# Moving the weights' split tiles, the pairs inside them and the sums of x to other places modulo 256 bytes

## The chip, the cores and the metric

One NeuronCore of a Trainium2 chip runs the whole kernel. The metric is the device time of one execution in microseconds (us), as the median of several executions. TensorE (PE in the profile) multiplies matrices: a weight load (LDWEIGHTS, shown as PEld) puts the stationary operand, 128 columns, into the array, and the MATMUL then streams the moving operand past it, 256 or 512 columns here. Both operands are read from SBUF, the on-chip memory of 128 partitions; an address below is a byte address within a partition. VectorE is DVE, ScalarE is ACT, GpSimd is POOL, and SyncE (SP) issues nearly all DMAs.

## The reference, cut to what matters

The input x is 256 tokens by 4096. The work is two normalisations, one big projection, a gated convolution, windowed attention, and one output projection:

```python
def hybrid_layer(x, w_in, conv_w, sink, w_out, ln_g, ln_b):
    p = x @ w_in                      # 256x4096 @ 4096x13312
...
    y_conv = c_b * centred_short_conv(c_c * c_h, conv_w) * jax.nn.silu(c_z)
    y_attn = banded_window_attention(a_q, a_k, a_v, sink) * jax.nn.silu(a_z)
    y = jnp.concatenate([y_conv, y_attn], axis=-1) @ w_out   # 4096x4096
    return layer_norm(DN_ALPHA * x + y, ln_g, ln_b)
```

All is float32. The projections hold nearly all of the arithmetic.

## The kernel before, in words

**How a product is made.** A float32 number is split in two float32r halves, a rounded one (hi) and the rest (lo), and a product is three matmuls: x-hi by w-hi, x-hi by w-lo, x-lo by w-hi. The tokens are the stationary operand, 128 at a time; the weights are the moving operand. Each of the 8.8 thousand matmuls has a weight load of its own. The tokens' halves lie in `xT`, 32 blocks of 2048 bytes, one for each 128 rows of the weights (`kt`), in each the 256 tokens' hi and then their lo, so a stationary block starts at a multiple of 512 bytes from the start of `xT`.

**The weights** come by DMA in tiles of 8192 bytes per partition (`w0` to `w2`, later `w6` to `w8` and parts of `R`). ACT makes the hi half of a tile (`split_hi`, tile `whi`) and DVE the lo half (`split_lo`, tile `wlo`), three buffers each, three steps ahead of the matmuls that use them. The code lists the order by hand: a list of steps, with a function for each that is emitted in the order of the list, so nothing is left to a scheduler.

**Three kinds of step.** A whole piece (lines 242 to 244 in the input projection, 908 to 910 in the output projection) multiplies four blocks of 512 columns by both token halves: 24 matmuls of 512 columns. A "half" step is the same with two blocks. In the last two chunks of the output projection (`CHUNKS` is 512 seven times and 256 twice) the blocks are 256 columns wide, on the same lines 908 to 910. A pair step (`mm_pair`, lines 266 to 268) does two blocks of 512 columns with seven products instead of eight, by a Strassen-like scheme: the DMA brings four blocks of 256 columns, DVE adds three or four more from them (`sums`, lines 181 to 183), and 21 matmuls of 256 columns follow. Of their stationary blocks three of seven are blocks of `xT` in the input projection's pairs, or four, and the others are sums of token blocks, kept in the tiles `SC`, `SC2` and, in the output projection, `SCy`.

**Where the tiles lie.** Pools take SBUF in the order in which they are opened, each tile rounded up to 32 bytes. `const` holds `ident`, `cw`, `sk`, `xT`, `musd` (32 bytes) and `eps_t` (4 bytes); behind it lie `wpool` (`whi`, `w0` to `w2`, `wlo`), then `small`, then the pools opened later: `psc` with the sums of x, `pw`, `pa` or `pc` (attention's tiles, convolution's tiles), `p2`. In a pair step the eight blocks of 1024 bytes lie at the tile's start plus 0 to 7 times 1024; block 0 of `whi` and `wlo` is not written, since block 0 only serves the sums (`part`, line 189).

Worked out from the code, the starts modulo 256 are: `ident` and `xT` 128; `whi`, `wlo`, `w0` to `w2` 192; `SC`, `SC2`, `SCy`, `R`, `w6` to `w8` and all of attention's tiles (`kT`, `v`, `qhl`, `pT`, `z`, `p`) 224.

Other matmuls: attention's scores (lines 551 to 553: moving `kT`, stationary `qhl`) and outputs (606 to 608: moving `pT`, stationary `v`), the first two pieces (line 369: `first` by `hT`, in plain float32, which takes two passes), and transposes (lines 334, 352, 481, 592: moving `ident`, stationary the tile that is turned).

Of the kernel before, what the change touches and what calls it, by code (L numbers as in the profile page):

```python
# [8 lines left out]
F32 = mybir.dt.float32  # L9
F32R = mybir.dt.float32r  # L10
AF = mybir.ActivationFunctionType
ALU = mybir.AluOpType
AX = mybir.AxisListType

P = 128
# [25 lines left out]
HW = W // 2  # L41
# [6 lines left out]
OP = 4  # L48
OUT_ORDERS = ["s" * 8] * 2 + ["sSsSsSsSss"] * 5 + ["", ""]
N_W = 3  # L50


def units(ci):
# [32 lines left out]
def npairs(ci):  # L86
    return PAIRS[ci] if ci < OUT else OUT_ORDERS[ci - OUT].count("S")
# [11 lines left out]
def encoder_kernel(ctx: ExitStack, tc: tile.TileContext, x, emb_g, emb_b, wi, ws, conv_w, sink, wo, ln_g, ln_b, out):  # L99
    nc = tc.nc  # L100
    PSUM = bass.MemoryType.PSUM

    const = ctx.enter_context(tc.tile_pool(name="const", bufs=1))
    wpool = ctx.enter_context(tc.tile_pool(name="wpool", bufs=3))
    small = ctx.enter_context(tc.tile_pool(name="small", bufs=4))
# [13 lines left out]
    is_pair = lambda j: steps[j][0] in ("pair", "opair")  # L119

    raw, wh, wl = {}, {}, {}
# [6 lines left out]
    def w_bufs(j):  # L128

        bs = [(wpool, f"w{k}") for k in range(N_W)] + (extra if j < N_IN else [])  # L130
        if j >= N_IN and R is not None:
            late = j > in_R[0][0]
            bs += [(None, name) for last, name in in_R if j <= last and late == (name == "R2")]
        last_user = lambda b: max(u for c, u in user.items() if c == b or b[1] == "R2" and c[0] is None) if (
            b in user or b[1] == "R2") else -1
        return min((last_user(b), k) for k, b in enumerate(bs)), bs

    def load(j, to=None):
        kind, a, b = steps[j]
        if to is None:  # L140
            (_, k), bs = w_bufs(j)
            pool, name = bs[k]
            user[bs[k]] = j
            if pool is None:
                to = raw[j] = {"R0": R[:, 0, D // 2:D], "R1": R[:, 1, D // 2:D], "R2": R[:, :, 3 * D // 4:D]}[name]
            else:
                to = raw[j] = pool.tile([P, PIECE], F32, name=name, bufs=1)
        src = {"in": (wi, IN_PIECES), "out": (wo, OUT_PIECES)}.get(kind, (ws, ALL_PAIRS))
        src = src[0][src[1].index((a, b))]
        if len(to.shape) == 3:  # L150
            if is_pair(j):
                nc.sync.dma_start(out=to[:, 0, :], in_=src)
            else:
                nc.sync.dma_start(out=to, in_=src.rearrange("p (i n) -> p i n", i=2))
        else:
            nc.sync.dma_start(out=to[:, 0:src.shape[1]], in_=src)

    def loads(j):

        nonlocal nxt  # L160
        while nxt < len(steps) and nxt <= j + 7:
            (u, _), bs = w_bufs(nxt)
            if u > j + (2 if len(bs) > N_W else 3):
                break
# [20 lines left out]
    def part(j, t):  # L185

        if len(raw[j].shape) == 3:
            return t if len(t.shape) == 3 else t.rearrange("p (i n) -> p i n", i=2)
        return t[:, HW:] if is_pair(j) else t[:, 0:4 * HW] if steps[j][0] == "half" else t

    def half_tile(j, name):
        if j < len(steps) - 1:
            return wpool.tile([P, PIECE], F32R, name=name)
        (_, k), bs = w_bufs(j)
        user[bs[k]] = j
        return bs[k][0].tile([P, PIECE], F32R, name=bs[k][1], bufs=1)

    def split_hi(j):
        wh[j] = half_tile(j, "whi")
        nc.scalar.activation(part(j, wh[j]), part(j, raw[j]), AF.Copy)  # L200

    def split_lo(j):
        wl[j] = half_tile(j, "wlo")
        nc.vector.tensor_tensor(part(j, wl[j]), part(j, raw[j]), part(j, wh[j]).bitcast(F32), op=ALU.subtract)  # L204
        raw.pop(j)

    def split(j):
        if j < len(steps):
            split_hi(j)
            split_lo(j)  # L210
# [7 lines left out]
    sk = const.tile([P, HEADS], F32, name="sk")  # L218

    xT = const.tile([P, KT, 2 * S], F32R, name="xT")  # L220
    musd = const.tile([P, 2, 4], F32, name="musd")
    eps_t = const.tile([P, 1], F32, name="eps_t")
    nc.vector.memset(eps_t, LN_EPS)


    acc = {}
# [21 lines left out]
    def mm_pair(j):  # L248


        _, ci, p = steps[j]
        hi, lo = (t.pop(j).rearrange("p (b w) -> p b w", w=HW) for t in (wh, wl))
        last = p == npairs(ci) - 1
        if p == 0:
            for k in range(2):
                pacc[ci, k] = ps_p.tile([P, 2, HW], F32, name="pacc")
        a, b = 2 * p, 2 * p + 1
        x = lambda kt, i: (xT[:, kt, i * HT:(i + 1) * HT], xT[:, kt, (2 + i) * HT:(3 + i) * HT])
        sc = lambda n: (SC[p][:, 0, n, :], SC[p][:, 1, n, :])
        p0, p1, c0, c1 = pacc[ci, 0], pacc[ci, 1], acc[ci, 0], acc[ci, 1]  # L260
        for (ah, al), w, o, opens, closes in (
                (x(a, 0), 2, p0[:, 0, :], True, False), (x(b, 0), 3, c0[:, 0:HW], False, False),
                (sc(2), 1, c0[:, HW:W], False, False), (x(b, 1), 7, c1[:, 0:HW], False, False),
                (sc(0), 5, p1[:, 1, :], True, False), (x(a, 1) if ci < OUT else sc(3), 6, p0[:, 1, :], False, True),
                (sc(1), 4, p1[:, 0, :], False, True)):
            nc.tensor.matmul(o, ah, hi[:, w, :], start=(opens and p == 0), stop=False)  # L266
            nc.tensor.matmul(o, ah, lo[:, w, :], start=False, stop=False)  # L267
            nc.tensor.matmul(o, al, hi[:, w, :], start=False, stop=(closes and last))  # L268


    def small_chain(i, dst):
# [10 lines left out]
    with tc.tile_pool(name="pro", bufs=1) as pro:  # L282
# [27 lines left out]
        nc.sync.dma_start(out=sk, in_=bass.AP(tensor=sink.tensor, offset=sink.offset, ap=[[0, P], [1, HEADS]]))  # L310
        for j in range(4, 2 + N_W):
            load(j)
# [89 lines left out]
        transp2(2, (1,))  # L402
        turned1(1, 0, t1[0])
        split_hi(2)
        first_mm(0, 1)
        transp2(3, (1,))
        turned1(1, 1, t1[1])
        first_mm(1, 1)
        turned2(2)
        split_lo(2)  # L410
        load(5)
        x_split(2)
# [380 lines left out]
    for j in range(n_pro, N_IN):  # L793
        kind, ci, q = steps[j]
        if j == z0 + 4:
            extra.clear()
        if j == z0 + 12:
            extra.insert(0, (pw, "w6"))
        mm_pair(j) if kind == "pair" else mm(j)
        split_hi(j + 3)  # L800
        for fn, a in later.pop(j, []):
            fn(*a)
        if kind == "pair" and q == PAIRS[ci] - 1:
            pair_copy(ci)
            at(j + 1, pair_sums, ci)
        if j in X_SUMS:
            x_sums(X_SUMS.index(j), pa.tile([P, 4 * S], F32, name="xs", tag="zT", bufs=2))
        if steps[j + 1][1] != ci or j == N_IN - 1:
            if ci == c_ch0:
                at(j + 10, open_pc)  # L810
            if PAIRS[ci]:
                at(j + (4 if j < N_IN - 1 else 1), chunk_end, j + 1, ci)
            else:
                chunk_end(j, ci)
        loads(j)
        sums(j + 4)
        split_lo(j + 3)
# [180 lines left out]
    for n, (c0, w, pk, j0) in enumerate(chunks):  # L998
        us = out_units(n)
        np_ = sum(u[0] == "opair" for u in us)  # L1000
        for t, (kind, _, q) in enumerate(us):
            j = j0 + t
            if kind == "opair":
                mm_pair(j)
            else:
                mm_out(j, n, (0,) if n == ncs - 1 else (0, 1))
# [114 lines left out]
```

## Time and profile before

| | us |
|---|---|
| median of 3 runs (lowest, highest) | 1534.17 (1534.01, 1534.74) |
| span of the profiled execution | 1532.5 |
| PE busy in it | 1518.5, 8879 matmuls |
| PEld busy | 1330.7 |
| DVE busy | 1329.9 |
| ACT busy | 780.7 |

The page gives the span, from the first to the last instruction; what lies around the span in the profiled execution is not listed apart, and the median of the runs stands 1.7 us above the span. PE is busy in every slice and its granted clock is 1.000. A MATMUL's listed duration includes its tail in the array, in which the next one has long begun (0.39 us for one that is followed after 0.23 us), so sums of durations say little; what counts is the distance from one start to the next, read from the timeline. Start times there are given to 0.01 us, so a distance is taken over many matmuls in a row.

### The profile page before, as it was taken

The page shows a single profiled execution, that of the slowest core. Times are in us where ns is not written, and L with a number is a line of the kernel's source. Part 1 is how long each engine was busy: PE and PEld are TensorE (multiplying, and loading weights), DVE is VectorE, ACT ScalarE, POOL GpSimd, SP SyncE. Part 2 cuts the span into 40 slices and gives each one's busy share as a digit, 9 for nine tenths or more (in the row PEclk, how much of TensorE's full clock was granted, in tenths as well). Part 3 has the DMA queues.
Part 4 walks back from the last instruction along what each step waited for, and adds up shares of the span by engine and source line. Part 5 has one row for each costly group of instructions (what it writes and reads, how often), then busy time and mean ns, then how long its engine had stood idle before and what let it go on. Part 6 is the DMA issues. An engine that isn't in the chain of part 4 may idle for free.

```text
span 1532.5 us, 21818 instructions
## 1 busy us (share of the span) xinstructions
PE 1518.5 (99%) x8879; PEld 1330.7 (87%) x8879; DVE 1329.9 (87%) x1555; ACT 780.7 (51%) x669; POOL 1.3 (0%) x7
## 2 busy tenths in 40 slices
PE   7999999999999999999999999999999999999998
PEld 4888889989998988889888889888988888888897
DVE  7769889899899898898898999989898688888876
ACT  4545546656566555545455445544456344443431
POOL 0000000000000000000000000000000000000000
PEclk9999999999999999999999999999999999999999
DMA  7545554555555555656555555556557756666663
GB/s 290 205 179 192 207 197 163 204 179 203 203 177 181 183 178 205 231 185 234 188 190 208 209 195 196 204 183 228 206 193 287 268 188 226 250 206 225 213 239 140
DMA packets 71716, 315.65 MB, mean 206 GB/s; under 512 B 8544, under 2 KB 12608, under 8 KB 50880
## 3 DMA queue, kind: packets, MB, share of 16 engines
q1 hardware_dynamic: 70608, 312.43, 57.2%
q10 hardware_dynamic: 1008, 1.84, 0.3%
q8 instruction: 69, 1.13, 0.3%
q14 instruction: 31, 0.25, 0.0%
HBM read 305.23 MB, written 8.91 MB: 205 GB/s over the span
## 4 chain that ended last, share of the span: by engine, by line
PE 96%; DVE 2%; DMA 1%; ACT 0%; SPq 0%; issue 0%; ACTq 0%
PE acc L242 15%; PE acc L243 15%; PE acc L244 15%; PE acc L908 6%; PE acc L910 6%; PE acc L909 6%; PE pacc L267 6%; PE pacc L266 6%; PE pacc L268 5%; PE acc L267 4%; PE acc L266 4%; PE acc L268 4%; PE att L481 1%; DVE wlo L204 1%; DMA w<-in_ws 0%; DVE st L319 0%
## 5 line engine op out<-in xcount | busy, mean ns | idle before, releaser
L200 ACT ACTIVATE whi<-w 128x2048 fp32r<-128x2048 f32 (+1 forms) x354 | 621.3, 1755 | 628.1 <-DVE w L183 213.5
L204 DVE TENSOR_TENSOR wlo<-w,whi 128x2048 fp32r<-128x2048 f32 (+1 forms) x354 | 736.5, 2083 | 129.3 <-ACT whi L200 128.8
L242 PE MATMUL acc<-whi,xT 128*128 128x512 f32 x988 | 391.1, 396 | 0.0
L243 PE MATMUL acc<-wlo,xT 128*128 128x512 f32 x988 | 387.6, 392 | 0.0
L244 PE MATMUL acc<-whi,xT 128*128 128x512 f32 x988 | 386.2, 391 | 0.0
L244 PEld LDWEIGHTS acc<-whi,xT 128*128 128x128 f32 x988 | 185.6, 188 | 41.5
L243 PEld LDWEIGHTS acc<-wlo,xT 128*128 128x128 f32 x988 | 185.6, 188 | 38.2 <-DVE wlo L204 1.7
L242 PEld LDWEIGHTS acc<-whi,xT 128*128 128x128 f32 x988 | 185.7, 188 | 36.1
L908 PE MATMUL acc<-whi,xT 128*128 128x512 f32 (+1 forms) x480 | 176.0, 367 | 0.0
L910 PE MATMUL acc<-whi,xT 128*128 128x512 f32 (+1 forms) x480 | 175.2, 365 | 0.0
L909 PE MATMUL acc<-wlo,xT 128*128 128x512 f32 (+1 forms) x480 | 174.6, 364 | 0.2 <-DVE wlo L204 0.2
L181 DVE TENSOR_TENSOR w<-w 128x512 f32<-128x512 f32 x179 | 122.3, 683 | 8.7 <-DMA w<-in_ws 8.7
L910 PEld LDWEIGHTS acc<-whi,xT 128*128 128x128 f32 x480 | 90.1, 188 | 15.7
L909 PEld LDWEIGHTS acc<-wlo,xT 128*128 128x128 f32 x480 | 90.1, 188 | 15.5 <-DVE wlo L204 0.9
L267 PE MATMUL acc<-wlo,xT 128*128 128x256 f32 x370 | 103.3, 279 | 0.0
L266 PE MATMUL acc<-whi,xT 128*128 128x256 f32 x370 | 103.1, 279 | 0.0
L268 PE MATMUL acc<-whi,xT 128*128 128x256 f32 x370 | 103.1, 279 | 0.0
L908 PEld LDWEIGHTS acc<-whi,xT 128*128 128x128 f32 x480 | 90.2, 188 | 14.0 <-issue 0.4
L266 PE MATMUL pacc<-whi,xT 128*128 128x256 f32 x350 | 99.4, 284 | 0.0
L267 PE MATMUL pacc<-wlo,xT 128*128 128x256 f32 x350 | 97.8, 279 | 0.0
L268 PE MATMUL pacc<-whi,xT 128*128 128x256 f32 x350 | 97.6, 279 | 0.0
L267 PE MATMUL pacc<-wlo,SC 128*128 128x256 f32 x330 | 93.0, 282 | 0.0
(230 smaller groups left out, 2055.2 us busy)
## 6 DMA issues: line engine op xcount, KB each, us to landing
w<-in_wi SPq DMA_DIRECT2D x112, 1024.0 KB
w<-in_ws SPq DMA_DIRECT2D x202, 512.0 KB
w<-in_wo SPq DMA_DIRECT2D x41, 1024.0 KB
R<-in_wo SPq DMA_DIRECT2D x13, 1024.0 KB
x<-in_x SPq DMA_DIRECT2D x7, 512.0 KB
yl<-yd SPq DMA_DIRECT2D x7, 512.0 KB
xc<-in_x SPq DMA_DIRECT2D x14, 256.0 KB
R<-in_ws SPq DMA_DIRECT2D x6, 512.0 KB
```

Of the source, the lines that this page charges most:

```text
L181: nc.vector.tensor_tensor(s01, b22, b12.to_broadcast([P, 2, HW]), op=ALU.add)
L200: nc.scalar.activation(part(j, wh[j]), part(j, raw[j]), AF.Copy)
L204: nc.vector.tensor_tensor(part(j, wl[j]), part(j, raw[j]), part(j, wh[j]).bitcast(F32), op=ALU.subtract)
L242: nc.tensor.matmul(a, xh, hk, start=(first and k == 0), stop=False)
L243: nc.tensor.matmul(a, xh, lk, start=False, stop=False)
L244: nc.tensor.matmul(a, xl, hk, start=False, stop=(last and k == PK - 1))
L266: nc.tensor.matmul(o, ah, hi[:, w, :], start=(opens and p == 0), stop=False)
L267: nc.tensor.matmul(o, ah, lo[:, w, :], start=False, stop=False)
L268: nc.tensor.matmul(o, al, hi[:, w, :], start=False, stop=(closes and last))
L908: nc.tensor.matmul(o, yh, hk, start=first, stop=False)
L909: nc.tensor.matmul(o, yh, lk, start=False, stop=False)
L910: nc.tensor.matmul(o, yl, hk, start=False, stop=last)
```

## The change

Three things are done, and no instruction is added, removed or moved: on every engine the same instructions stand in the same order with the same waits, and only addresses differ.

- `musd` and `eps_t` go from `const` to `small`, which takes 64 bytes from in front of `wpool`: `whi` and `wlo` (and `w0` to `w2`) now start at 128 modulo 256, as `xT` does.
- An unused tile `gap` of 160 bytes in `small`, with the two tiles that moved there, moves every later pool up by 160 bytes: `SC`, `SC2`, `SCy`, `R`, `w6` to `w8` and attention's tiles go from 224 to 128 modulo 256.
- A pair's halves are written `SHIFT` = 48 elements, 192 bytes, lower in their tile than before (`dst`): block w then starts at the tile's start plus 1024 w minus 192, which is 192 modulo 256, where it was before. `mm_pair` reads blocks by `w - 1` from a view that starts there. The branch for a raw tile with two rows is taken by no pair step of this kernel: all 3885 matmuls of the pairs read at 192 modulo 256.

The offset of the moving block from the stationary block, modulo 256, is then:

| matmuls | lines before | offset before | offset after |
|---|---|---|---|
| 512 columns, `whi`/`wlo` by `xT` | 242 to 244, 908 to 910 | 64 | 0 |
| pairs, by `xT` | 266 to 268 | 64 | 64 |
| pairs, by `SC`, `SC2`, `SCy` | 266 to 268 | 224 | 64 |
| 256 columns of the last two chunks | 908 to 910 | 64 | 0 |
| attention | 551 to 553, 606 to 608 | 0 | 0 |
| transposes of tiles at 224 | 352, 481, 592 | 160 | 0 |

`first` by `hT` (line 369) goes from 224 to 0. 

```diff
+SHIFT = 48
...
+    def dst(j, t):
+
+        return t[:, HW - SHIFT:8 * HW - SHIFT] if is_pair(j) and len(raw[j].shape) == 2 else part(j, t)
...
     def split_hi(j):
         wh[j] = half_tile(j, "whi")
-        nc.scalar.activation(part(j, wh[j]), part(j, raw[j]), AF.Copy)
+        nc.scalar.activation(dst(j, wh[j]), part(j, raw[j]), AF.Copy)
 
     def split_lo(j):
         wl[j] = half_tile(j, "wlo")
-        nc.vector.tensor_tensor(part(j, wl[j]), part(j, raw[j]), part(j, wh[j]).bitcast(F32), op=ALU.subtract)
+        nc.vector.tensor_tensor(dst(j, wl[j]), part(j, raw[j]), dst(j, wh[j]).bitcast(F32), op=ALU.subtract)
+        if is_pair(j):
+            c0 = HW if len(raw[j].shape) == 3 else HW - SHIFT
+            wh[j], wl[j] = wh[j][:, c0:c0 + 7 * HW], wl[j][:, c0:c0 + 7 * HW]
         raw.pop(j)
...
     xT = const.tile([P, KT, 2 * S], F32R, name="xT")
-    musd = const.tile([P, 2, 4], F32, name="musd")
-    eps_t = const.tile([P, 1], F32, name="eps_t")
+    musd = small.tile([P, 2, 4], F32, name="musd", bufs=1)
+    eps_t = small.tile([P, 1], F32, name="eps_t", bufs=1)
     nc.vector.memset(eps_t, LN_EPS)
+    small.tile([P, 40], F32, name="gap", bufs=1)
...
-            nc.tensor.matmul(o, ah, hi[:, w, :], start=(opens and p == 0), stop=False)
-            nc.tensor.matmul(o, ah, lo[:, w, :], start=False, stop=False)
-            nc.tensor.matmul(o, al, hi[:, w, :], start=False, stop=(closes and last))
+            nc.tensor.matmul(o, ah, hi[:, w - 1, :], start=(opens and p == 0), stop=False)
+            nc.tensor.matmul(o, ah, lo[:, w - 1, :], start=False, stop=False)
+            nc.tensor.matmul(o, al, hi[:, w - 1, :], start=False, stop=(closes and last))
```

## The prediction

> **What bounds the kernel now.** First the page's busy times and the chain that ended last.
>
> ```profile
> PE 1518.5 (99%) x8879; PEld 1330.7 (87%) x8879; DVE 1329.9 (87%) x1555; ACT 780.7 (51%) x669; POOL 1.3 (0%) x7
> PE 96%; DVE 2%; DMA 1%; ACT 0%; SPq 0%; issue 0%; ACTq 0%
> ```
>
> TensorE is the bound: 96% of the chain is PE. The view of waits says whether PE is held up by anyone.
>
> ```profile
> ACT whi L200 <- PE acc L244: 176.9, 80, 3.9
> PE att L382 <- DMA x<-in_x: 8.7, 1, 8.7
> ```
>
> The longest wait of PE in that view is 8.7 us, once, at the start. The other way round, ACT waits 176.9 us for PE to free the hi tiles, so the splits run ahead of the matmuls. A saving in the distance between two matmuls is therefore a saving in time, until DVE is late. How near DVE is, by stage:
>
> ```profile
> core 0: us, PE busy (x) PEld busy (x) DVE busy (x) ACT busy (x) POOL busy (x), PEclk, DMA share, GB/s
> 330.00:600.00 270.00, 269.65 (x1693) 242.46 (x1692) 248.04 (x319) 162.35 (x186) 0.00 (x0) 1.00 0.53 184
> 600.00:1160.00 560.00, 560.00 (x3400) 499.90 (x3399) 508.22 (x556) 287.00 (x194) 0.00 (x0) 1.00 0.58 207
> ```
>
> DVE is busy 248 of 270 us in the attention stage and 508 of 560 in the convolution stage. PE could become 8% faster there before DVE's work alone is longer.
>
> So the question is the distance from one matmul to the next. The listing by form gives the counts of the 512-column matmuls.
>
> ```profile
> L242 PE MATMUL acc<-whi,xT 128*128 128x512 f32 x988 | 391.1, 396 | 0.0
> L243 PE MATMUL acc<-wlo,xT 128*128 128x512 f32 x988 | 387.6, 392 | 0.0
> L244 PE MATMUL acc<-whi,xT 128*128 128x512 f32 x988 | 386.2, 391 | 0.0
> L908 PE MATMUL acc<-whi,xT 128*128 128x512 f32 x368 | 144.8, 393 | 0.0
> L910 PE MATMUL acc<-whi,xT 128*128 128x512 f32 x368 | 144.3, 392 | 0.0
> L909 PE MATMUL acc<-wlo,xT 128*128 128x512 f32 x368 | 143.6, 390 | 0.2 <-DVE wlo L204 0.2
> ```
>
> These are 3 x 988 + 3 x 368 = 4068 matmuls. The timeline of PE gives their distance, here from the first and last row of two undisturbed stretches.
>
> ```profile
> 192.89 0.40 PE L242 MATMUL acc<-whi,xT 128*128 128x512 f32 x1
> 203.85 0.40 PE L244 MATMUL acc<-whi,xT 128*128 128x512 f32 x1
> 1187.24 0.40 PE L909 MATMUL acc<-wlo,xT 128*128 128x512 f32 x1
> 1263.70 0.39 PE L910 MATMUL acc<-whi,xT 128*128 128x512 f32 x1
> ```
>
> From 1187.24 to 1263.70 there are 334 distances: 228.9 ns each, and nearly all stretches show this number. The stretch from 192.89 to 203.85, with 47 distances at the same offset, shows 233.2. What would it be without any disturbance? The plain float32 matmuls take the same 512 columns in two passes:
>
> ```profile
> 23.65 3.60 PE L369 MATMUL acc<-first,hT 128*128 128x512 f32 x8
> 27.09 0.60 PE L352 MATMUL att<-ident,x 128*128 128x128 f32 x4
> ```
>
> Eight of them take 3.44 us, 430 ns each. Half of it, 215 ns, is my estimate of 512 columns streamed once with nothing in the way: 0.42 ns a column. So each 512-column matmul carries about 14 ns too much, 57 us in all. The 256-column matmuls, in the same view:
>
> ```profile
> 457.69 0.28 PE L606 MATMUL att<-pT,v 128*128 128x256 f32 x1
> 458.29 0.28 PE L608 MATMUL att<-pT,v 128*128 128x256 f32 x1
> 1159.20 0.28 PE L266 MATMUL pacc<-whi,xT 128*128 128x256 f32 x1
> 1164.03 0.28 PE L268 MATMUL pacc<-whi,SC 128*128 128x256 f32 x1
> 1473.78 0.28 PE L908 MATMUL acc<-whi,xT 128*128 128x256 f32 x1
> 1503.58 0.28 PE L910 MATMUL acc<-whi,xT 128*128 128x256 f32 x1
> 1504.02 0.28 PE L910 MATMUL acc<-w,xT 128*128 128x256 f32 x1
> 1512.15 0.28 PE L910 MATMUL acc<-whi,xT 128*128 128x256 f32 x1
> ```
>
> Attention, offset 0: 5 distances of 120.0 ns. Two pair steps, offsets 64 and 224 mixed: 41 distances of 117.8. The last chunks, all at offset 64: 263 distances of 113.3, and then, after one wait, 69 of 117.8 with the very same offsets. So the offset is not the whole story: at offset 64 there are two states, and a wait can throw PE from one into the other. All these numbers are multiples of 6.67 ns over one matmul or over three (17, 18 and 35 times 6.67 is 113.3, 120.0 and 233.3; 53 thirds are 117.8; 103 thirds are 228.9), and 6.67 ns is the time of 16 columns, 64 bytes, at 0.42 ns.
>
> **A picture that fits the rows.** The next weight load runs beside the stream. Transposes, whose moving operand has only 128 columns, follow each other at the pace of the load:
>
> ```profile
> 1186.29 0.87 PE att L481 x8
> 1519.91 3.12 PE pacc L1057 x28
> ```
>
> That is 108.8 ns for a load of 128 columns, half the stream's speed. Both read SBUF. While a load reads 512 bytes the stream reads 1024, so it gains 512 bytes, twice 256. If places equal modulo 256 collide, stream and load meet twice in each load, each meeting costing the stream about one 64-byte step: 2 x 6.67 = 13.3, near the 14 seen. In the plain float32 matmuls both run at the same speed and never meet, and at 430 they show no more than twice 215. The second row above, `ident` by `ident` at offset 0 (111.4 ns against 108.8), shows what offset 0 does at the start: the load loses a few ns.
>
> **The change part by part.**
>
> *512 columns, offset 64 to 0.* Stream and load now start at the same place, the stream just ahead, so the first meeting is at the start (paid by the load, which has 100 ns of slack under 512 columns), the second in the middle, and the third would fall where the load ends. One inner meeting is left of two: 6.67 ns less, 222.2 instead of 228.9. 4068 x 6.67 = **27.1 us less**. No row shows 512 columns at offset 0. The ends of what is possible: all 14 ns gone (57 us less), and the 233.3 of the slow stretch (4.4 x 4068 = 18.1 us more). I take one meeting, since attention at offset 0 fits it: 108.8 + 6.67 for one meeting + some 4 for the load's late start, which 256 columns cannot hide, is 119.5, against 120.0 seen.
>
> *Pairs.* The matmuls by `xT` keep offset 64; those by the sums go from 224 to 64. The two together average 117.8, which is also one of the two states of pure offset 64. **0 us** is what I take; if the quick state holds, 3885 x 4.45 = 17.3 us less; if they fell to 120.0, 8.6 us more. I take 0 because the pairs come in steps of 4.8 us between whole pieces, waits and transposes, and the row behind a wait shows 117.8.
>
> *The 256-column matmuls of the last two chunks* are whole pieces and not shifted: offset 64 to 0, where attention shows 120.0. 264 x 6.67 + 120 x 2.2 = **2.0 us more**.
>
> *Transposes.* 264 of them come to offset 0: 264 x 2.6 = **0.7 us more**, by the two rows above. Attention's matmuls stay at offset 0.
>
> *DVE and ACT* write and read at other places. Two sources with different places modulo 256 (192 for w, 224 for R) show whether they care:
>
> ```profile
> L204 DVE TENSOR_TENSOR wlo<-w,whi 128x1792 fp32r<-128x1792 f32 x179 | 361.0, 2020 | 43.1 <-ACT whi L200 42.9
> L204 DVE TENSOR_TENSOR wlo<-R,whi 128x1792 fp32r<-128x1792 f32 x6 | 12.1, 2021 | 3.1 <-ACT whi L200 3.1
> ```
>
> 2020 against 2021 ns: they don't. 0 us. They stay hidden: 1.8% less time leaves DVE at some 93% in the attention stage. If that cover went, the bound would be DVE's 248 and 508 us, far below.
>
> *Sum:* -27.1 + 2.0 + 0.7 = -24.4 us on the span of 1532.5, so 1508.1; the median of the runs lies 1.7 us above the span, so **1509.8 us**.
>
> **A rule that speaks against it.** The Trainium skill, "TensorE: Matmul & The Clock Gate", in "Part 2: What happens when you issue a matmul", says that PE has two independent read ports: "Loading the next tile's weights doesn't steal SBUF read bandwidth from the running matmul." By that rule the offset would change nothing. The trace disagrees in part: 113.3, 117.8 and 120.0 ns for the same shape, though the first two share their offsets.
>
> **The rivals.**
>
> *One meeting less and the pairs in the quick state:* 1509.8 - 17.3 = 1492.5. For it: 263 distances of 113.3 in a row, directly behind 512-column matmuls. Against: pairs at `xT` follow 512 columns too and show 117.8. Chance 0.16.
>
> *512 columns at offset 0 still meet at the load's end,* and pay what attention pays above the estimate, 11 ns in place of 14: 34 steps, 226.7. That is 2.2 x 4068 = 9.0 us less, with the 2.7 more, 1527.9. Chance 0.18.
>
> *It doesn't do what it says:* the excess belongs to the stream itself or to its phase, not to the offset. For it: two states at one offset, and pairs whose mixed offsets average what offset 64 alone does. The 512 columns stay at 228.9, nothing moves by more than the 2.7 us: 1534 to 1537. This is also what the skill's rule gives. Chance 0.13.
>
> *Slower:* at offset 0 both start on the same place in each of the 4068 matmuls, and the stream, not the load, loses that first step: the 35 steps of the slow stretch, 233.3, become the rule. 18.1 + 2.0 + 0.7 more: 1555. For it: the rows at offset 0 are the slowest of their kinds (120.0 and 111.4). It decides as soon as the 512-column distance is above 228.2, where the 2.7 us are no longer paid for. Chance 0.17.
>
> **How the numbers follow.** The forecast, one meeting less, has 0.36, its own range 1504 to 1516. Faster by over 0.2% (3 us, about what a measurement of this kernel can tell from no change) is 0.36 + 0.16 + 0.18 = 0.70; the same 0.13; slower 0.17. The range that leaves out two in ten reaches from 1488, below the quick pairs, to 1540, past no change and short of the slow rival.
>
> **What would show it.** In the timeline after, the distance of 512-column matmuls: 222.2 is right, 226.7 the second rival, 228.9 the third, 233.3 the last. The pairs' distance: 117.8, or 113.3. The last chunks: 120.0. L481 in eights: 0.89. DVE's means must stay. I'd be wrong above all if stream and load do not collide by their places modulo 256, or if the load wins where they start together; and if PE's saving is real but waits for DVE's `wlo` appear in front of it.

## The result and the profile after

| | before | after |
|---|---|---|
| median of 9 runs (lowest, highest), us | 1534.69 (1533.81, 1535.49) | 1530.89 (1530.31, 1531.13) |
| span of the profiled execution, us | 1532.5 | 1529.3 |
| ratio, 95% interval | | 0.9976 [0.9967, 0.9985] |

The change makes the kernel 3.8 us faster. The forecast was 1509.8, 24 us faster: the direction was right, the size was not. 1530.89 lies inside the stated range, which was wide enough to hold no change as well. The page of after has the head, the busy times (share of the span, x instructions) and the chain that ended last:

```profile
span 1529.3 us, 21818 instructions
PE 1515.3 (99%) x8879; PEld 1332.8 (87%) x8879; DVE 1330.2 (87%) x1555; ACT 782.1 (51%) x669; POOL 1.3 (0%) x7
PE 98%; DMA 1%; DVE 1%; ACT 0%; SPq 0%; issue 0%; ACTq 0%
```

The view of waits of after (engine and line that waits, who is waited for: us in total, times, longest) shows that PE is still the bound. ACT waits for PE as before, and the weight loads of line 252 waited for DVE's `wlo` 2.5 us in all.

```profile
ACT whi L205 <- PE acc L253: 178.2, 81, 3.7
PEld acc L252 <- DVE wlo L209: 2.5, 10, 0.3
```

In before the same loads, there of line 243, had waited 1.7 us:

```profile
PEld acc L243 <- DVE wlo L204: 1.7, 7, 0.3
```

So the distances between matmuls tell the rest. The timeline of PE in after (start, duration, engine, line, operation), first the ends of three undisturbed stretches:

```profile
1184.64 0.39 PE L917 MATMUL acc<-whi,xT 128*128 128x512 f32 x1
1259.89 0.39 PE L919 MATMUL acc<-whi,xT 128*128 128x512 f32 x1
...
1156.91 0.28 PE L277 MATMUL acc<-whi,xT 128*128 128x256 f32 x1
1161.15 0.28 PE L277 MATMUL pacc<-whi,SC 128*128 128x256 f32 x1
...
1469.60 0.28 PE L919 MATMUL acc<-whi,xT 128*128 128x256 f32 x1
1508.48 0.28 PE L919 MATMUL acc<-whi,xT 128*128 128x256 f32 x1
```

The 512-column matmuls: 332 distances in 75.25 us, 226.7 ns each (before 228.9). A pair step: 36 distances of 117.8. The last chunks: 324 of 120.0 (before 113.3 and 117.8). The next piece of the same timeline is what the forecast had not thought of, the first 512-column matmuls behind that pair step:

```profile
1161.27 0.40 PE L251 MATMUL acc<-whi,xT 128*128 128x512 f32 x1
1161.51 0.39 PE L252 MATMUL acc<-wlo,xT 128*128 128x512 f32 x1
1161.73 0.39 PE L253 MATMUL acc<-whi,xT 128*128 128x512 f32 x1
1161.96 0.40 PE L251 MATMUL acc<-whi,xT 128*128 128x512 f32 x1
1162.20 0.39 PE L252 MATMUL acc<-wlo,xT 128*128 128x512 f32 x1
1162.43 0.40 PE L253 MATMUL acc<-whi,xT 128*128 128x512 f32 x1
1162.66 0.39 PE L251 MATMUL acc<-whi,xT 128*128 128x512 f32 x1
1162.89 0.39 PE L252 MATMUL acc<-wlo,xT 128*128 128x512 f32 x1
```

Their distances, from the unrounded starts, are 241, 224, 231, 236, 228, 232 and 231 ns, and only then 226 and 227. After each of its 125 entries into 512 columns the kernel pays such a settling. Averaged over all entries, the distances 3 to 11 hold 23 ns more than nine at pace; in before they held 3 ns more. The first two distances are long in both traces, 506 ns together, so they gained nothing from the shorter pace.

The 8878 distances between neighbouring matmuls, summed by kind in both traces, give the account below. "At pace" is the mean of those not held up by a wait (up to 245 ns for 512 columns, 126 ns for 256).

| us in all (mean at pace, ns) | before | after | difference | forecast |
|---|---|---|---|---|
| 512 columns, 4068 | 937.8 (229.3) | 931.7 (227.7) | -6.1 | -27.1 |
| pairs, 3885 | 459.0 (117.7) | 459.6 (117.9) | +0.6 | 0 |
| last two chunks, 384 | 44.6 (114.7) | 46.5 (119.9) | +1.9 | +2.0 |
| transposes, 264 | 25.6 | 25.9 | +0.3 | +0.7 |
| attention, 192 | 24.8 | 25.4 | +0.6 | 0 |
| others | 27.5 | 27.3 | -0.2 | 0 |
| first to last matmul | 1519.4 | 1516.5 | -2.9 | -24.4 |

### The profile page after: what moved, and what is told of

It reads as the page before. It is cut to its first block, busy times and chain, and to the rows that moved or that the text cites. A ratio compares the mean times of both kernels' runs of the same rounds, so it can differ in the third digit from the quotient of the medians.

```text
span 1529.3 us, 21818 instructions
## 1 busy us (share of the span) xinstructions
PE 1515.3 (99%) x8879; PEld 1332.8 (87%) x8879; DVE 1330.2 (87%) x1555; ACT 782.1 (51%) x669; POOL 1.3 (0%) x7
## 4 chain that ended last, share of the span: by engine, by line
PE 98%; DMA 1%; DVE 1%; ACT 0%; SPq 0%; issue 0%; ACTq 0%
PE acc L252 15%; PE acc L251 15%; PE acc L253 15%; PE acc L917 7%; PE acc L918 6%; PE acc L919 6%; PE pacc L275 6%; PE pacc L277 6%; PE pacc L276 6%; PE acc L275 4%; PE acc L277 4%; PE acc L276 4%; PE att L490 1%; DMA x<-in_x 1%; PE att L601 1%; PE acc L378 0%
## 5 line engine op out<-in xcount | busy, mean ns | idle before, releaser
L275 PE MATMUL pacc<-whi,SC 128*128 128x256 f32 x330 | 92.4, 280 | 0.0
```

Of the source, the lines that this page charges most:

```text
L275: nc.tensor.matmul(o, ah, hi[:, w - 1, :], start=(opens and p == 0), stop=False)
```

## The experiments

Three measuring kernels and six variants ran. Offset means the start of the moving block less that of the stationary block, modulo 256 bytes. The kernel before was run again beside each group; its medians were 1535.27 to 1535.67.

**What does each offset cost by itself?** A measuring kernel without the computation, only stretches of 60 matmuls, each stretch behind four transposes:

```python
OFFS = list(range(0, 256, 16))
...
    for o in OFFS:
        stretch(512, o)
    for o in OFFS:
        stretch(256, o)
    for m in (96, 64, 32):
        for o in (0, 64, 128, 192):
            stretch(512, o, m)
```

Here `m` is the number of columns loaded.

> A kernel of its own: it leaves out the whole computation and only runs stretches of 60 float32r matmuls, each with its weight load, four transposes between stretches, no work on the other engines beside them. 16 stretches of 512 columns with the moving block 0, 16, ... 240 bytes past the stationary block modulo 256, 16 the same with 256 columns, then 512 columns with a stationary block of 96, 64 and 32 columns at offsets 0, 64, 128, 192. Theory 1 (stream and load collide where their places agree modulo 256, one 6.67 ns step for each meeting): at 64 bytes 228.9 and at 0 226.7 as in the two kernels, one range of offsets with a whole step less (about 222) and the others near 229; with 64 stationary columns the load is half as long, one meeting, 7 ns less than with 128; with 32 columns nearly no excess, about 217. Theory 2 (a toll on each matmul that does not come from the load, rounded up to the 6.67 ns grid, the place only sets the rounding): every offset between 226.7 and 233.3, and 64 or 32 stationary columns change nothing.

Each stretch is one row in the timeline, and the row of the transposes behind it gives its end:

```profile
70.87 14.00 PE L46 MATMUL a<-mv,st 128*128 128x512 f32 x60
84.71 0.60 PE L40 MATMUL tr<-ident,xs 128*128 128x128 f32 x4
...
113.81 13.86 PE L46 MATMUL a<-mv,st 128*128 128x512 f32 x60
127.51 0.60 PE L40 MATMUL tr<-ident,xs 128*128 128x128 f32 x4
...
477.59 14.13 PE L46 MATMUL a<-mv,st 128*32 128x512 f32 x60
491.56 0.60 PE L40 MATMUL tr<-ident,xs 128*128 128x128 f32 x4
```

Offset 64 takes 13.84 us, offset 112 takes 13.70, and offset 0 with only 32 columns loaded 13.97. The first distance in each of the three is some 315 ns. The means of the last 30 distances of each stretch, in ns:

| offset | 0 | 16 | 32 | 48 | 64 | 80 | 96 | 112 |
|---|---|---|---|---|---|---|---|---|
| 512 columns | 226.7 | 231.6 | 233.3 | 233.3 | 228.9 | 231.1 | 233.3 | 226.7 |
| 256 columns | 120.0 | 116.7 | 117.8 | 118.4 | 117.8 | 120.0 | 120.0 | 113.3 |

| offset | 128 | 144 | 160 | 176 | 192 | 208 | 224 | 240 |
|---|---|---|---|---|---|---|---|---|
| 512 columns | 232.3 | 233.3 | 234.2 | 233.3 | 233.3 | 234.7 | 233.3 | 226.7 |
| 256 columns | 118.7 | 118.7 | 118.7 | 119.2 | 113.3 | 119.2 | 118.3 | 117.2 |

The kernel's values come back: 228.9 and 117.8 at 64, 226.7 and 120.0 at 0. So the places alone make them, with no DMA and no DVE at work and ACT only at a stretch's end. 222.2 stands nowhere. The settling of 512 columns at offset 0 can't be read here: that stretch is the first of the kernel, and its first seven distances are 418 to 591 ns. In the two later measuring kernels, where other stretches stand ahead, it does come back: distances of up to 232 and 236 ns among the first nine, then 226 and 227. The loads of fewer columns are shorter:

```profile
L46 PEld LDWEIGHTS a<-mv,st 128*128 128x128 f32 x1920 | 294.5, 189 | 43.7 <-ACT mv L35 2.6
L46 PEld LDWEIGHTS a<-mv,st 128*32 128x32 f32 x240 | 26.1, 109 | 28.5
```

In this listing by form the means are 189 and 109 ns, and a block of 32 columns is 128 bytes, half of the period of 256. By the forecast's picture it meets the stream once at most, yet its 512-column stretches stay at 230.7 to 231.7 ns at all four offsets; loads of 96 and 64 columns gave 228.3 to 233.4. The number of meetings within a load does not set the toll, the excess of a distance over the bare stream.

**Does the toll grow with the columns?** The same measuring kernel, again without the computation, with other widths: `for o in (112, 64, 0): for w in (128, 192, ..., 504, 512): stretch(w, o)`.

> The same measuring kernel (it leaves out the whole computation) with stretches of 128, 192, 256, 320, 384, 448, 480, 496, 504 and 512 columns at the offsets 112, 64 and 0. Theory 2 (a fixed toll for each matmul, then rounded up to the next 6.67 ns): with 0.417 ns a column and a toll of some 8 ns, at offset 112: 109 for 128 and 192 columns (the load's pace), 113.3 for 256, 146.7 for 320, 173.3 for 384, 200.0 for 448, 213.3 for 480, 220.0 for 496 and 504, 226.7 for 512; at 64 and 0 the same or one step more. Theory 1b (the toll grows with the columns, since the stream itself loses time along its way): 320 at 140.0 and 384 at 166.7 with a toll of one step, 512 with two.

| columns | 192 | 256 | 320 | 384 | 448 | 480 | 496 | 504 | 512 |
|---|---|---|---|---|---|---|---|---|---|
| offset 0 | 111.7 | 120.0 | 146.7 | 173.3 | 202.7 | 216.7 | 223.4 | 226.7 | 226.7 |
| offset 64 | 111.7 | 117.8 | 146.7 | 173.3 | 200.0 | 218.2 | 226.7 | 228.9 | 228.9 |
| offset 112 | 111.6 | 113.3 | 146.8 | 173.3 | 206.7 | 213.3 | 226.7 | 236.5 | 231.1 |

128 columns took 111.7 at offsets 0 and 64, as 192 did. From 256 to 384 columns offset 0 grows by 53.3 ns for 128 columns, 0.4167 ns a column; taken as the stream's own pace this is 213.3 for 512. Above it offset 0 costs 13.3 ns at 256, 320, 384 and 512 columns, and 16 to 17 at 448 to 504. The other two offsets rise and fall with the width, 11 to 20 ns at 64 and 7 to 27 at 112. So the toll does not grow steadily with the columns, as theory 1b had it, but one fixed toll, rounded up, does not give these rows either. The same offset 112 gave 226.7 in the first measuring kernel and 231.1 here, so an offset has several states.

**The parts of the change.** First without the pairs' shift (they come to offset 0 too): `SHIFT = 0` instead of 48.

> The changed kernel with SHIFT = 0: the pairs' halves stay where they were in their tiles, so all pairs read at offset 0. If the pairs' shift is worth what attention's 120.0 ns at offset 0 says, the pairs go from 117.8 to 120.0: 3885 x 2.2 = 8.6 us more than the changed kernel, 1539.5. If the offset does nothing to pairs among other work, 1531.

1535.27 us (1534.98 to 1535.92), ratio to before 0.9998 [0.9989, 1.0008]: without the shift nothing of the gain is left. The pairs go to 119.75 ns at pace, 466.8 us in all, 7.2 more than after, near the 8.6 expected; the 512s take 2.1 less than there, which the expectation had not. Next the sums alone: only the gap is added to the kernel before, `small.tile([P, 40], F32, name="gap", bufs=1)`.

> The kernel before with the gap of 160 bytes alone: weights stay at offset 64 from xT, only the pairs' sums (and the tiles of the later pools) come onto the grid, offset 224 to 64. Theory 1 with the trace's 117.8 for both: no change, 1534.7 within 1. If pairs at pure offset 64 can hold the quick state of 113.3 behind 512-column matmuls at offset 64: up to 17 us less, some 1518 to 1530.

1534.72 us, ratio 0.9993 [0.9984, 1.0003]: no measurable change. The pairs fall by 3.3 us to 116.9 ns at pace, the 512s rise by 2.2 and the last chunks by 1.1. The last chunks stand at 117.8 at pace in place of 114.7, though their operands lie where they lay: another of their states. In 40 of the 185 pair steps, all now at offset 64, the distances average 113 ns, and in after, where the pairs have the same offset, in none. What differs ahead of them is the offset of the 512-column matmuls, 64 here and 0 there.

**Other places for the pairs.** The first measuring kernel had 113.3 ns at offsets 192 and 112: `SHIFT = 16` and `SHIFT = 36` instead of 48.

> The changed kernel with SHIFT = 16: pairs at offset 192 from xT and from the sums, where the measuring kernel showed 113.3 at once; whole pieces stay at 0. If the table of offsets carries over to the kernel: the pairs go from 117.8 to 113.3, 3885 x 4.45 = 17.3 us less than the changed kernel, 1513.6. Rival (the phase at entry, behind whole pieces, waits and transposes, decides the state, not the place): pairs stay near 117.8, 1529 to 1533.

1529.45 us (1528.96 to 1529.88), ratio to before 0.9964 [0.9951, 0.9977]. At offset 192 some 600 pair distances are 113.3 to 113.6, and some 3100 are 117.7 to 117.8: the quick state exists, but most steps run in the other, and the time is the rival's.

> The changed kernel with SHIFT = 36: pairs at offset 112, where the measuring kernel came to 113.3 only after 11 distances of some 119. A run of pairs is 21 or 42 matmuls long, so if each run pays that settling: 17.3 us less, and some 125 x 11 x 5.5 ns = 7.6 us of it given back, about 1521. Without settling 1513.6. Rival (entry decides): 1529 to 1533.

1526.48 us (1526.12 to 1527.15), ratio 0.9947 [0.9930, 0.9963]. This is the quickest version that was run, quicker than both kernels, and between the two expectations. Its timeline, from one matmul to another 20 distances later in one pair step:

```profile
1154.98 0.28 PE L275 MATMUL pacc<-whi,xT 128*128 128x256 f32 x1
1157.25 0.28 PE L277 MATMUL pacc<-whi,SC 128*128 128x256 f32 x1
```

That is 113.5 ns. Over the kernel the pairs take 447.9 us, 11.7 less than after, yet the matmul stretch is only 5.1 us shorter (1511.4). Its waits name one taker:

```profile
PEld acc L252 <- DVE wlo L209: 8.0, 27, 0.7
PE acc L252 <- DVE wlo L209: 1.5, 4, 0.4
PE att L601 <- DVE s L567: 1.7, 4, 0.4
```

A weight load that uses a `wlo` waited 2.5 us in after and waits 8.0 here. The 512s take 4.7 us more than after, though their pace is no worse (227.6), and attention takes 2.1 more. The loss stands at the entries: of their first two distances 74 are over 245 ns, 51 in after, and these take 5.3 us more than there. So DVE's cover gives out at the entries, well before DVE is busy all the time (511 of 560 us in the convolution stage).

**All at 112?** `xT` and the sums 16 bytes later in their tiles, the weights' tiles at 0 modulo 256, no shift:

```diff
-    xT = const.tile([P, KT, 2 * S], F32R, name="xT")
+    xT = const.tile([P, KT * 2 * S + 4], F32R, name="xT")[:, 4:].rearrange("p (k t) -> p k t", k=KT)
...
-SHIFT = 48
+SHIFT = 0
```

> The changed kernel with everything at offset 112: xT and the sums start 16 bytes later in their tiles, the weights' tiles at 0 modulo 256, pairs not shifted (four small tiles are merged in twos to make room). 512 columns at 226.7 without the settling of the first eight distances (some 2.8 us less than the changed kernel), the last chunks at 113.3 instead of 120.0 (2.4 us less), pairs at 113.3 (17.3 us less, or some 10 with settling): 1508 to 1516. Rival (DVE and ACT are late once PE is 1.5% faster): waits for wlo appear in front of PE and the time stays above 1520.

1552.22 us (1551.50 to 1553.65), ratio 1.0115 [1.0100, 1.0130]: slower, 17 us over before, and not by the rival's cause: the loads' waits for `wlo` are 0.7 us in all. The ends of 21 distances in its timeline:

```profile
1155.57 0.39 PE L254 MATMUL acc<-whi,xT 128*128 128x512 f32 x1
1160.47 0.39 PE L254 MATMUL acc<-whi,xT 128*128 128x512 f32 x1
```

233.3 ns at offset 112, where 226.7 or 231.1 had been measured with stationary blocks at multiples of 256. So more than the difference counts, or the state is another.

**Whose place counts?** A third measuring kernel, without the computation, also moves the stationary block by `s` bytes past a multiple of 256, and repeats one stretch three times at its end.

> A measuring kernel: it leaves out the whole computation and runs stretches of 60 matmuls of 512 or 256 columns, each stretch behind four transposes. This time the stationary block starts 0, 16, 32, 64 or 128 bytes past a multiple of 256, and the moving block 0, 64, 112, 192 or 240 bytes further on. Theory 1, only the difference modulo 256 counts: the five places of the stationary block give one distance at each difference, those of the first measuring kernel, for 512 columns 226.7 at 0, 228.9 at 64, 226.7 at 112, 233.3 at 192, 226.7 at 240, for 256 columns 120.0, 117.8, 113.3, 113.3, 117.2, each within 1 ns. Theory 2, each block's own place modulo 64 counts as well (the kernel with x 16 bytes later had 233.3 and 116.7 or 120.0 at difference 112): places 0, 64 and 128 agree with the first measuring kernel, and places 16 and 32 give other values by 3 to 7 ns at one difference at least, 233.3 for 512 columns and 116.7 or 120.0 for 256 at place 16 and difference 112. Theory 3, neither place decides but the moment at which a stretch begins: the last three stretches, which repeat 512 columns at place 0 and difference 112, differ among themselves or from the same stretch before by over 3 ns.

| 512 columns: offset | 0 | 64 | 112 | 192 | 240 |
|---|---|---|---|---|---|
| s = 0 | 226.7 | 228.9 | 231.1 | 233.3 | 236.7 |
| s = 16 | 231.1 | 226.7 | 233.2 | 228.9 | 233.3 |
| s = 32 | 226.7 | 228.9 | 231.1 | 233.3 | 236.7 |
| s = 64 | 226.7 | 228.9 | 231.1 | 233.3 | 236.7 |
| s = 128 | 226.6 | 228.9 | 231.1 | 233.3 | 233.3 |

Place 16 differs from place 0 at every offset, and places 0, 32, 64 and 128 agree at the first four: the stationary block's place counts besides the difference, and 32 bytes were no different from 0, where theory 2 expected them to be. 16 is the only place off the multiples of 32 that was tried. The 233.3 of the kernel with everything at 112 is the 233.2 of place 16. For 256 columns at offset 112 it is the same, 118.4 at place 16 and 113.3 at the others; at offset 192 all five places gave 113.3, and at 64 places 0 and 64 gave 117.8 and the rest 113.3. The state is real as well. Its timeline has place 0 and offset 112 first within the table and then in three repetitions; here the first and the second repetition:

```profile
169.38 14.11 PE L47 MATMUL a<-mv,st 128*128 128x512 f32 x60
183.33 0.60 PE L40 MATMUL tr<-ident,xs 128*128 128x128 f32 x4
...
585.40 13.85 PE L47 MATMUL a<-mv,st 128*128 128x512 f32 x60
599.09 0.60 PE L40 MATMUL tr<-ident,xs 128*128 128x128 f32 x4
```

13.95 us the first time and 13.69 here, by the same 60 instructions: 231.1 and 226.7 ns. The other two repetitions took 231.1. At places 0, 32, 64 and 128, 512 columns settled at 226.7 at offset 0 and at 228.9 at offset 64.

**The weights' move alone, beside quick pairs.** The weights' tiles are back at offset 64, the pairs stay at 112:

```diff
-SHIFT = 48
+SHIFT = 52
...
     xT = const.tile([P, KT, 2 * S], F32R, name="xT")
+    const.tile([P, 16], F32, name="gap0")
...
-    small.tile([P, 40], F32, name="gap", bufs=1)
+    small.tile([P, 24], F32, name="gap", bufs=1)
```

> The kernel with the pairs at offset 112, but with the weights' tiles back where they were before the change: the 512-column matmuls and those of the last two chunks at offset 64 again, pairs at 112, sums and attention as after the change. Theory 1, the 512s' move brought about what the traces show, a steady distance 2.2 ns shorter and a settling behind each entry: the 512s have 228.9 from the second or third distance on, some 1.2 us more than in the kernel with pairs at 112 alone; the last chunks fall from 120.0 to 113 to 118, 2.1 us less; the pairs stay at 114 to 116; in all 1525.6. Rival, the pairs' state is set by the phase in which the 512s end: the pairs fall back to 117.8 or 120.0 in most steps, 3 ns or more for some 3600 of them, and the time is 1536 or more.

1531.37 us (1530.65 to 1531.74), ratio 0.9972 [0.9962, 0.9983]. Neither expected time came. What theory 1 says of the 512s is borne out: with the weights back their pace is 2 ns longer again, and the distances 3 to 11 behind an entry hold 5 ns more than nine at 228.9, where the kernel with moved weights holds 21 more than nine at 226.7. The pairs kept their quick state (115.0 at pace), but the time is 4.9 us above that of the kernel with pairs at 112 and moved weights. In the traces the 512s make 5.5 of it (941.9 against 936.4 us), by their pace: 229.5 against 227.6 ns, with fewer waits for `wlo` (4.6 against 8.0 us). The 1.2 us expected is about what the 512s of before (937.8) cost above those 936.4, but in before the loads of line 243 waited 1.7 us for `wlo`, against 8.0 in the kernel with moved weights. Here the pace, 1.9 x 4068 = 7.7 us, outweighs what the fewer waits give back. Some stretches at offset 64 also fall into a slow state of 233 ns, above all those behind attention: eight stretches with 208 distances, against four with 104 in before.

## Why the prediction came out as it did

- **PE is the bound, and a shorter distance is time won: right.** The chain is 98% PE, and the account by distances (-2.9 us) agrees with the spans (-3.2).
- **512 columns, -27.1 us: the step that failed.** "One inner meeting is left of two: 6.67 ns less, 222.2 instead of 228.9." The pace fell to 226.7, by 2.2 ns: 34 steps of 6.67 ns, the value of the rival that kept the last meeting. The picture from which the step came does not hold: loads of 32 columns do not lower the toll, and offset 0 pays the same 13.3 ns at 256 and at 512 columns, while from offset 0 to 64 the one falls (120.0 to 117.8) and the other rises (226.7 to 228.9). The fit of 119.5 to attention rested on five distances; attention's mean at pace over all of before is 118.7, and the "some 4" in it, the load's late start, had no row behind it.
- **The 215 ns of a bare stream: near, by luck.** The 16 plain float32 matmuls of the code stand as 32 rows at line 369, so a row of 430 ns is one of the two passes, and nothing in the traces says to halve it once more. The widths of the second measuring kernel give 213.3 by another way.
- **The settling was missing.** 2.2 x 4068 = 9.0 us would have been the rival's gain. 125 entries with some 20 ns more than before (23 - 3) take 2.5 us of it back, and the first two distances, no shorter than before, another 0.5. That leaves 6.0, against the 6.1 of the account. The rival's 1527.9 plus these 3.0 is 1530.9, and 1530.89 was measured; so close a match is partly luck, since the small terms of the account are each off by some tenths.
- **Pairs, 0: right in the sum** (+0.6 us), and the reason given, that they stay in the 117.8 state, is what the timeline shows. Without the shift, which was no case of the prediction, the pairs cost 7.2 us more, and the time is that of before.
- **Last chunks, +2.0: right** (+1.9), 120.0 throughout.
- **Transposes, +0.7: wrong in kind, and too small to matter.** In the chain eight of them still take as long as before, where 0.89 was forecast:

```profile
1183.23 0.87 PE att L490 x8
```

- **DVE and ACT, 0: right.** In after's listing by form the same split takes the same time, 2020 ns:

```profile
L209 DVE TENSOR_TENSOR wlo<-w,whi 128x1792 fp32r<-128x1792 f32 x179 | 361.2, 2020 | 43.2 <-ACT whi L205 43.2
```

The 8% of room that the prediction reads from DVE's busy time is an average, though: with the pairs at 112 the kernel is 0.6% faster than before, and the loads of line 252 wait 8.0 us for `wlo`.

- **The rule of two independent ports** (the Trainium skill, "TensorE: Matmul & The Clock Gate", Part 2) would have left the time as it was. The measuring kernels disagree on the outcome: the same instructions on the same amounts of data take from 226.7 to 236.7 ns by their places alone. That it is the load which disturbs the stream is argued and not shown, since no run here streams float32r without loading, and the loads of 32 columns, which did not lower the toll, speak against it.

What stays open is why a place costs what it costs, and what in an entry picks the state.

## What to carry over

Where one engine's pace is the bound and a term of the sum is a distance that no row shows, measure that distance by itself before it is multiplied by thousands: one kernel of bare stretches gave the 226.7 and the 120.0 together. A steady pace is not the whole cost of a stretch; with 125 entries, the first eleven distances took back a third of the gain. And a saving on the bound goes on only as long as the cover of the next engine holds at each single entry: 11.7 us won in the pairs became 5.1.

## What the runs showed of the hardware that was not expected

- The distance of float32r matmuls depends on the operands' places in SBUF: 512 columns 226.7 to 236.7 ns, 256 columns 113.3 to 120.0 ns, with nothing else running. The offset modulo 256 counts, and the stationary block's own place: 16 bytes past a multiple of 256 gave other values than place 0 at all five offsets for 512 columns, 32 and 64 bytes past it gave the same.
- Many steady distances are multiples of 6.67 ns (16 columns) over one, two or three matmuls: 226.7 is 34 steps, 228.9 is 103 thirds, 231.1 is 104 thirds, 236.7 is 71 halves. Others in the tables, such as 231.6, 234.2 and 118.7, are not.
- Several states belong to one offset: 113.3 and 117.8 for 256 columns at 64, 226.7 and 231.1 for 512 columns at 112. In these stretches a distance, once settled, lasted to the stretch's end.
- A shorter load does not help: with 32 instead of 128 columns it takes 109 instead of 189 ns, and the matmuls' distance stays at 230.7 to 231.7.
